# Decoder trunk: top-k selection by signs on ScalarE, and the threshold search with its branch traced ahead of the gated attention

## The chip, the cores and the metric

The kernel runs on one core of a Trainium2 chip, as one launch. The metric is the device time of that launch in microseconds (us), the median over several runs. TensorE is called PE here and its weight loads PEld; VectorE is DVE, ScalarE is ACT, GpSimd is POOL, SyncE is SP.

## The reference, cut to what matters

A trunk of two layers on 1024 tokens of width 1024, with 16 meta tokens put ahead (1040 rows in all). Each layer runs two groups of heads on the same normalised stream. Group A is gated linear attention (GLA), four heads in chunks. Group B is sparse attention: an indexer scores all earlier keys for every query, the 256 best are kept, and softmax attention runs over those. Both outputs are gated, concatenated and projected.

```python
def _layer(h, ...):
    proj = jnp.einsum('bld,de->ble', h, w_in)
    g_q, g_k, g_v, g_lr, g_z, a_q, a_k, a_v, i_q, i_k, i_w, a_z = _split_cols(proj)
    o_gla = _gla(gq, gk, gv, glog) ...          # group A, chunks of 64
    o_dsa = _dsa(aq, ak, av, iq, ik, i_w, S) * silu(a_z)
    y = concat([o_gla, o_dsa]) @ w_out
    return _layer_norm(DEEPNORM_ALPHA * h + y, ln_g, ln_b)

def one_block(inp):                             # 128 queries of _dsa
    dots = einsum('bqjd,bsd->bqjs', iqb, ik) * (IDX_HD ** -0.5)
    score = einsum('bqj,bqjs->bqs', iwb * (IDX_HEADS ** -0.5), relu(dots))
    score = where(causal, score, -inf)
    _, sel = lax.top_k(score, topk)             # topk = 256
    ...                                         # softmax over the 256 keys kept
```

## The kernel before, in words

Everything is float32, with each float32 factor split into a rounded part and a remainder, so that one projection is three passes on PE. The whole layer lives in on-chip memory; DRAM scratch holds projections that are needed in another layout.

The stages of a layer, in the order in which they are written:

- **index scores**: index projections, `index_scores` (PE dots, ACT Relu at L535, DVE weighted sum at L540) give `score[i]` for the query blocks i = 1 to 7, side by side in the tile `r_sc`; block i has 144 + 128 i columns (272, 400, ... 1040; 4592 in all).
- **GLA**: `gla_proj(f)` for the two halves f = 0, 1 (projections `wgqk` at L353 to L355 and `gvp` at L567 to L569), and `gla(f)`: a short chunk of 16 tokens, then two of 512. For each of up to seven levels DVE subtracts (L622, L624), ACT takes exponentials (L625, L628), POOL multiplies (L626, L632), PE multiplies into the tile `lev` (L639), and DVE copies under a mask (L643). The results go to `go` and `ms`.
- **attention projections**: `wak`, `waq`, `wav` (`proj_fm`, L353 to L355), with rotary embedding. The gates `wz` (`proj_z`) come from the same lines; they are traced between the attention's units at every second unit (`ZX`).
- **threshold search**, DVE: statistics of each score row, then five rounds of counts over all seven blocks (`count`, L753) with a secant step of [128x7] operations between them (L809 to L819), then `finish` (L772, L774, L776: the eight largest remaining values give the exact threshold). A matmul by ones (`fail`, L824) says whether any row still misses its count by more than 8. A branch inside a `tile_critical` (L828) repeats the search bit by bit in that case. All engines take part in that branch: DVE waits for the other engines and for the DMA queues, loads the flag, compares, and lets the others go on.
- **selection** (L861 to L873): for each block DVE counts the scores above the threshold (L866), marks the ties (L867), numbers them with a scan (L868), keeps the first ones (L870) and writes a 0/1/2 code into the score (L871); POOL scales it to a bias in bf16 (L872) and adds the causal mask (L873).
- **attention**: `va` and `ak` are made ready (transposes `vT` at L885, the split of `ak` at L896 and L897), then 32 units of two heads: `stage_a` (PE scores `S` at L1022, DVE adds the bias at L1023 and reduces, ACT exponential at L1029) and `stage_b` (PE transposes `PT` at L1047, ACT and DVE split them at L1050 and L1051, PE `o` at L1053 and later).
- **output projection and LayerNorm.**

The order on each engine is not the written one: a scheduler orders the instructions of all engines by priority and by its own estimate of when operands are there. Priority follows the written order; `tc.high_priority(offset=...)` moves a piece ahead. Each engine then runs its own list strictly in order. The search is written behind the attention projections with an offset of 1 (`TPRI`); DVE gets to it early since its operands are there, and its instructions end up among those of GLA.

Of the kernel before, what the change touches and what calls it, by code (L numbers as in the profile page):

```python
# [24 lines left out]
L = 1040  # L25
# [71 lines left out]
def trunk(ctx: ExitStack, tc, a, out, dbg=None, stop=None):  # L97
# [82 lines left out]
    V.memset(halves, 0.0)  # L180
    for o in range(2):
        V.memset(halves[64 * o:64 * o + 64, o:o + 1], 1.0)
    zcol = small(2)
    V.memset(zcol[:, 0:1], 0.0)
    V.memset(zcol[:, 1:2], 1.0)
    zero_b = zcol[:, 0:1]
# [222 lines left out]
    for l in range(DEPTH):  # L409
# [296 lines left out]
        s1 = slot(0, F32, "rope")
        ropeb = [s1[:, 520 * x:520 * x + 520] for x in range(2)]
        proj_fm(proj_dram(wfm[AK], ak_dram, 0, "wak"))
        rope_dram(ak_dram, 0, ropeb[0], KRA)
        for j in range(4):  # L710
            proj_fm(proj_dram(wfm[AQ + j], aq_dram, j, "waq", -0.125))
            rope_dram(aq_dram, j, ropeb[1 - j % 2], KRA)
        avr = s1[:, 2 * L:3 * L]

        def ev(c, n, p):
            S.activation(avr[:, c:c + n], p, AF.Copy)
        proj_fm((wfm[AV], 128, "wav", ev))

        def proj_z(j):
            def ev(c, n, p):  # L720
                if j < 4:
                    gt = unit("zu")[:, :n]
                    Q.dma_start(gt, g_dram[j, :, c:c + n])
                if j in ZDVE:
                    e = unit("zu")
                    V.tensor_scalar(e[:, :n].bitcast(I32), p.bitcast(I32), -(1 << 31), None, OP.bitwise_or)
                    S.activation(e[:, :n], e[:, :n], AF.Exp)
                    S.activation(e[:, :n], e[:, :n], AF.Ln, bias=one_b, scale=1.0)
                else:
                    e = log_sigmoid_parts(p, 0.0, 128, n, "zu")  # L730
                V.scalar_tensor_tensor(e[:, :n], p, 0.0, e[:, :n], OP.min, OP.subtract)
                S.activation(e[:, :n], e[:, :n], AF.Exp)
                if j < 4:
                    V.scalar_tensor_tensor(e[:, :n], p, ng, e[:, :n], OP.mult, OP.mult)
                    G.tensor_tensor(e[:, :n], e[:, :n], gt, OP.mult)
                else:
                    V.tensor_tensor(e[:, :n], p, e[:, :n], OP.mult)  # L737
                S.dma_start(z_dram[j, :, c:c + n], e[:, :n])
            proj_fm((wfm[GZ + j], 128, "wz", ev))

        for j in ZORD[:ZPRE]:
            proj_z(j)


        bias = {0: causal}
        for i in range(1, NB):
# [40 lines left out]
            V.tensor_tensor(sel_v, sel_v, selcap, OP.min)  # L787
            dr()

        with tc.high_priority(offset=TPRI):  # L790
            mean, sd, sl, sl_lo, sl_hi, dl = sel_w[5:11]
            th, er = sel_t, sel_e
            for i in blks:
                V.bn_stats(sel_st[:, i - 1, :], score[i][:, :min(SELN, 16 + 128 * i)])
                V.bn_aggr(sel_mv[:, i - 1, :], sel_st[:, i - 1:i, :])
            S.activation(sd, sel_mv[:, :, 1], AF.Ln, bias=eps_c, scale=1.0)
            S.activation(sd, sd, AF.Exp, scale=0.5)
            V.tensor_tensor(mean, sd, selz, OP.mult)
            V.tensor_tensor(th[0], sel_mv[:, :, 0], mean, OP.add)
            V.tensor_tensor(sl, sd, selc, OP.mult)  # L800
            V.tensor_scalar(sl_lo, sl, 0.25, None, OP.mult)
            V.tensor_scalar(sl_hi, sl, 4.0, None, OP.mult)
            for k in range(NSEC):
                t, e = th[k % 2], er[k % 2]
                count(e, t, OP.is_ge, 0.5 - TOPK)
                if k == NSEC - 1:
                    break
                nt, ok = th[1 - k % 2], sel_w[11]
                V.scalar_tensor_tensor(ok, e, -1.0, e, OP.mult, OP.max)  # L809
                V.tensor_scalar(ok, ok, 8.0, None, OP.is_lt)  # L810
                if k:
                    V.scalar_tensor_tensor(sl, er[1 - k % 2], 0.25, e, OP.add, OP.subtract)
                    V.reciprocal(sl, sl)
                    V.tensor_tensor(sl, sl, dl, OP.mult)
                    V.tensor_tensor(sl, sl, sl_lo, OP.max)
                    V.tensor_tensor(sl, sl, sl_hi, OP.min)
                V.tensor_tensor(dl, e, sl, OP.mult)
                V.tensor_tensor(nt, t, dl, OP.add)
                V.copy_predicated(nt, ok.bitcast(I32), t)  # L819

            V.scalar_tensor_tensor(sel_w[11], e, -1.0, e, OP.mult, OP.max)
            V.scalar_tensor_tensor(sel_w[11], sel_w[11], 8.0, selact, OP.is_gt, OP.mult)
            pf = tr("fail")
            T.matmul(pf[:, :7], ones, sel_w[11], start=True, stop=True)  # L824
            finish(e)
            V.tensor_reduce(sel_w[11][:1, 0:1], pf[:1, :7], axis=AX.X, op=OP.max)
            V.tensor_scalar(sel_f, sel_w[11][:1, 0:1], 0.0, None, OP.is_gt)
            with tc.tile_critical(sync_engine=mybir.EngineType.DVE):  # L828
                left = V.value_load(sel_f)
                with V.If(left != 0):  # L830

                    cnt, neg, acc, z0 = er[0], er[1], sel_w[11], sel_w[10]
                    mt, ct = th[0].bitcast(I32), th[1].bitcast(I32)
                    V.memset(z0, 0.0)
                    V.drain()
                    count(cnt, z0, OP.is_ge, 0.0)
                    V.drain()
                    V.tensor_scalar(neg, cnt, float(TOPK), None, OP.is_lt)
                    V.drain()
                    V.tensor_copy(mt, neg)  # L840
                    V.drain()
                    V.tensor_scalar(mt, mt, 31, None, OP.logical_shift_left)
                    V.drain()
                    for bit in range(30, -1, -1):
                        V.tensor_scalar(ct, mt, 1 << bit, None, OP.bitwise_or)
                        V.drain()
# [12 lines left out]
            cnt = er[0]
            for i in blks:  # L860
                W = 144 + 128 * i  # L861
                t = sel_v[:, i - 1:i]
                rr[5] = 1 - rr[5]
                oz = r_oz[:, rr[5]]
                eq, cs = oz[:, :260].bitcast(U8), oz[:, 260:780].bitcast(I16)
                V.tensor_scalar(bias[i], score[i], t, float(-TOPK), OP.is_gt, OP.add, accum_out=cnt[:, i - 1:i])  # L866
                V.tensor_scalar(eq[:, :W], score[i], t, None, OP.is_equal)  # L867
                V.tensor_tensor_scan(cs[:, :W], eq[:, :W], zero_b.to_broadcast([128, W]), cnt[:, i - 1:i],  # L868
                                     OP.add, OP.add)
                V.scalar_tensor_tensor(eq[:, :W], cs[:, :W], 0.0, eq[:, :W], OP.is_gt, OP.mult)  # L870
                V.scalar_tensor_tensor(score[i], score[i], t, eq[:, :W], OP.is_lt, OP.add)  # L871
                G.tensor_scalar(bias[i], score[i], BIG, 0.0, OP.mult, OP.add)  # L872
                G.tensor_tensor(bias[i][:, W - 128:W], bias[i][:, W - 128:W], causal[:, 16:144], OP.add)  # L873

        vat = [slot(1, F32R, "va"), slot(3, F32R, "vb")]
        va = []
# [305 lines left out]
def _tables():  # L1182
# [24 lines left out]
    for p in range(128):  # L1207
        for i in range(1, NB):
            nv = 17 + 128 * i + p
            z = NormalDist().inv_cdf(max(5e-3, 1 - TOPK / nv))  # L1210
            seltab[p, i - 1] = z
            seltab[p, 6 + i] = np.sqrt(2 * np.pi) / (nv * max(np.exp(-z * z / 2), 0.15))
            seltab[p, 13 + i] = BIG if nv >= TOPK else -BIG
            seltab[p, 20 + i] = nv >= TOPK
    seltab[:, 28:] = np.arange(8) + 0.5
    return {"ident": np.eye(128, dtype=np.float32), "causal": causal, "mcaus": mcaus, "lmask": lmask,
# [43 lines left out]
```

## Time and profile before

| | us |
|---|---|
| median of 3 runs | 1513.29 (1512.71 to 1514.68) |
| profiled execution, its own time | 1515.28 |
| span of that execution | 1513.5 |
| PE busy | 1386.8 (92%) |
| DVE busy | 1061.5 (70%) |
| ACT busy | 762.6 (50%) |
| POOL busy | 723.3 (48%) |

PE is the busiest engine. "Busy" counts the time in which an instruction of the engine ran; a group line gives the engine, the operation, output and input tiles with their sizes, the count, the busy time and the mean of one in ns, and behind the second bar the idle time just before, with what ended it. The granted clock (PEclk) is given as a share of 2.4 GHz: 1.00 is that level throughout, 0.5 is 1.2 GHz.

### The profile page before, as it was taken

Reading aid. Unit: us, or ns where it says so; the run is one execution under the profiler, and the core shown is the slowest. Engines: PE = TensorE matmul, PEld = TensorE weight load, DVE = VectorE, ACT = ScalarE, POOL = GpSimd, SP = SyncE. Lnnn points to the kernel's source line nnn. Section 1 sums busy time; section 2 is a strip of 40 time slices with the busy share of each in tenths; the row PEclk is TensorE's granted clock in tenths of the full one; section 3 lists DMA queues with packets and bytes.
Section 4 is the critical chain, followed back from the end, with each engine's and each line's share of the span. In section 5 each row is a group of like instructions: output and inputs, shape, how many; then the busy total and the mean of one; then the engine's idle time right before and its main releaser. Section 6 shows DMA issues by size and latency. Waiting matters only on the chain. (4 is left out here: it accounts for less than half of the span.)

```text
span 1513.5 us, 27140 instructions
## 1 busy us (share of the span) xinstructions
PE 1386.8 (92%) x9471; PEld 1290.6 (85%) x9471; DVE 1061.5 (70%) x2465; ACT 762.6 (50%) x1745; POOL 723.3 (48%) x690
## 2 busy tenths in 40 slices
PE   2988998999968999999999899999997899999985
PEld 2888897898958998898998889888897799899985
DVE  8569999565197556776497699994624955778638
ACT  5446623343355777653254573334434577876412
POOL 6533346596344546322363442866923644652134
PEclk9999999999978999999999999999998899999988
DMA  7242331242423446215233432314242253631422
GB/s 250 102 141 82 91 116 50 86 127 83 129 64 92 136 132 163 66 48 158 75 126 116 124 98 81 107 58 127 83 131 64 65 147 106 183 109 52 153 67 112
DMA packets 143166, 162.63 MB, mean 107 GB/s; under 512 B 19552, under 2 KB 112496, under 8 KB 143024
## 3 DMA queue, kind: packets, MB, share of 16 engines
q1 hardware_dynamic: 112656, 125.73, 27.9%
q10 hardware_dynamic: 30368, 35.12, 6.8%
q8 instruction: 75, 1.23, 0.3%
q14 instruction: 67, 0.55, 0.1%
HBM read 104.76 MB, written 56.04 MB: 106 GB/s over the span
## 5 line engine op out<-in xcount | busy, mean ns | idle before, releaser
L320 POOL TENSOR_TENSOR w<-w 128x512 fp32r<-128x512 f32 (+1 forms) x134 | 179.4, 1339 | 299.6 <-ACT w L319 232.5
L319 ACT ACTIVATE w<-w 128x512 fp32r<-128x512 f32 (+1 forms) x134 | 83.4, 624 | 108.7 <-DMA w<-in_w_fm_dram 58.4
L353 PE MATMUL wz<-X,w 128*128 128x346 f32 (+1 forms) x384 | 130.5, 340 | 2.3 <-DVE zu L737 1.8
L540 DVE SCALAR_TENSOR_TENSOR r_sc<-v,cst,r_sc 128x346 f32<-128x346 f32 (+6 forms) x196 | 125.0, 693 | 6.3 <-ACT v L535 5.2
L354 PE MATMUL wz<-X,w 128*128 128x346 f32 (+1 forms) x384 | 129.3, 337 | 0.0
L355 PE MATMUL wz<-X,w 128*128 128x346 f32 (+1 forms) x384 | 129.3, 337 | 0.0
L1051 DVE TENSOR_TENSOR u<-PT,u 128x512 fp32r<-128x512 f32 (+1 forms) x160 | 100.4, 632 | 30.1 <-ACT u L1050 21.3
L1050 ACT ACTIVATE u<-PT 128x512 fp32r<-128x512 f32 (+1 forms) x160 | 85.9, 544 | 61.9 <-PE PT L1047 60.4
L1029 ACT ACTIVATE r_g<-r_g,cst 128x272 f32<-128x272 f32 (+7 forms) x128 | 99.7, 779 | 20.1 <-DVE cst L1023 19.8
L632 POOL TENSOR_TENSOR qb<-r_g,u 64x256 f32<-64x256 f32 (+1 forms) x144 | 104.2, 724 | 5.8
L1022 PE MATMUL S<-ak,aq 128*128 128x346 f32 (+7 forms) x240 | 81.9, 348 | 18.8 <-DVE ak L897 10.3
L567 PE MATMUL gvp<-w,X 128*128 128x256 f32 (+1 forms) x288 | 83.3, 291 | 9.5 <-DVE r_g L643 8.0
L535 ACT ACTIVATE v<-dots 128x346 f32<-128x346 f32 (+5 forms) x224 | 85.8, 457 | 12.2 <-PE dots L533 8.5
L1047 PE MATMUL PT<-cst,r_g 128*128 128x128 f32 x576 | 89.2, 278 | 1.1 <-DVE cst L1023 1.1
L568 PE MATMUL gvp<-w,X 128*128 128x256 f32 (+1 forms) x288 | 83.4, 290 | 0.0
L569 PE MATMUL gvp<-w,X 128*128 128x256 f32 (+1 forms) x288 | 82.8, 288 | 0.0
L353 PEld LDWEIGHTS wz<-X,w 128*128 128x128 f32 x384 | 76.4, 199 | 3.9 <-DVE zu L737 2.3
L354 PEld LDWEIGHTS wz<-X,w 128*128 128x128 f32 x384 | 76.7, 200 | 0.3
L355 PEld LDWEIGHTS wz<-X,w 128*128 128x128 f32 x384 | 76.4, 199 | 0.4
L1117 PE MATMUL yp<-w,X 128*128 128x256 f32 (+1 forms) x238 | 69.9, 295 | 6.0 <-ACT X L1087 6.0
L643 DVE COPY_PREDICATED r_g<-cst,lev 128x512 f32<-128x512 uint8 (+1 forms) x72 | 52.5, 729 | 32.0 <-PE lev L639 31.4
L1022 PE MATMUL S<-ak 128*128 128x346 f32 (+7 forms) x240 | 74.8, 320 | 0.0
(348 smaller groups left out, 4900.6 us busy)
## 6 DMA issues: line engine op xcount, KB each, us to landing
w<-in_w_fm_dram SPq DMA_DIRECT2D x88, 256.0 KB
r_g<-aq_dram SPq DMA_DIRECT2D x64, 128.0 KB
w<-in_w_out_dram SPq DMA_DIRECT2D x32, 256.0 KB
r_sc<-h_dram SPq DMA_DIRECT2D x53, 128.0 KB
h_dram<-r_g SPq DMA_DIRECT2D x12, 512.0 KB
r_dram<-r_sc SPq DMA_DIRECT2D x48, 128.0 KB
r_sc<-z_dram SPq DMA_DIRECT2D x22, 256.0 KB
z_dram<-zu ACTq DMA_DIRECT2D x32, 173.0 KB
```

The costliest lines, as they stand in the source:

```text
L320: G.tensor_tensor(lo[:, :n], raw[:, :n], hi[:, :n].bitcast(F32), OP.subtract)
L353: T.matmul(p[:m, :n], wh, xh, start=(k == 0), stop=False)
L354: T.matmul(p[:m, :n], wh, xl, start=False, stop=False)
L355: mm = T.matmul(p[:m, :n], wl, xh, start=False, stop=(k == 7))
L535: S.activation(rl[:, :n], p[:, :n], AF.Relu)
L540: V.scalar_tensor_tensor(sco[:, c:c + n], rl[:, :n], w, sco[:, c:c + n], OP.mult, OP.add)
L632: eng.tensor_tensor(qb[P, :, o].rearrange("p c (b m) -> p c b m", m=m), qv[P, :, 1, :].rearrange("p (c b) m -> p c b m", c=nch), Ev[P, :, ...
L1022: mm = T.matmul(p[:, :n], q[x][:, h % 4, :], ak[g][:, c:c + n], start=(x == 0), stop=(x == 1))
L1029: ins = S.activation(P[:, :W], P[:, :W], AF.Exp, bias=mx[:, h, nci - 1:nci], scale=-1.0, accum_out=mx[:, h, 4:5]).ins
L1047: T.transpose(p[:, 256 * x + 128 * hh:256 * x + 128 * hh + 128], Pt[hh][:, 128 * (k0 + x):128 * (k0 + x) + 128], ident)
L1050: S.activation(ph[:, :256 * kk], p[:, :256 * kk], AF.Copy)
L1051: V.tensor_tensor(pl[:, :256 * kk], p[:, :256 * kk], ph[:, :256 * kk].bitcast(F32), OP.subtract)
```

## The change

1. **The search moves.** Search and branch become a function that is called right behind the index scores, ahead of `gla_proj(0)`; all of GLA and the attention projections are written behind it. The `fail` matmul, its reduction and the branch get an offset of 4000 (`FPRI`), and `fail` has a PSUM bank of its own.
2. **The selection changes.** For each block ACT takes the sign of score minus threshold (with its sum) and the square of the sign (with its sum); two DVE operations of [128x1] work out how many ties fit; a DVE scan numbers the ties from these (bf16 in, minus one per column that isn't a tie); one DVE operation joins sign and number into an integer; ACT turns it into the bias with a Relu scaled by minus `BIG`. POOL has no part any more. Causally masked columns carry a score of about minus `BIG`, so their sign masks them. The selection stays behind the projection code, with an offset of 1 (`SELPRI`).

```diff
+SELPRI = 1
+FPRI = 4000
...
-    zcol = small(2)
+    zcol = small(3)
+    V.memset(zcol[:, 2:3], -1.0)
...
-        gla_proj(0)
-        gla(0)
-        gla_proj(1)
-        gla(1)
...
-        with tc.high_priority(offset=TPRI):
+        def search():
+            with tc.high_priority(offset=TPRI):
+                search_()
+
+        def search_():
...
-            pf = tr("fail")
-            T.matmul(pf[:, :7], ones, sel_w[11], start=True, stop=True)
+            with tc.high_priority(offset=FPRI):
+                pf = bank("fl", 1, "fail")
+                T.matmul(pf[:, :7], ones, sel_w[11], start=True, stop=True)
             finish(e)
-            V.tensor_reduce(sel_w[11][:1, 0:1], pf[:1, :7], axis=AX.X, op=OP.max)
-            V.tensor_scalar(sel_f, sel_w[11][:1, 0:1], 0.0, None, OP.is_gt)
-            with tc.tile_critical(sync_engine=mybir.EngineType.DVE):
+            with tc.high_priority(offset=FPRI):
+                V.tensor_reduce(sel_w[11][:1, 0:1], pf[:1, :7], axis=AX.X, op=OP.max)
+                V.tensor_scalar(sel_f, sel_w[11][:1, 0:1], 0.0, None, OP.is_gt)
+            with tc.high_priority(offset=FPRI), tc.tile_critical(sync_engine=mybir.EngineType.DVE):
...
+        search()
+        gla_proj(0)
+        gla(0)
+        gla_proj(1)
+        gla(1)
...
+        with tc.high_priority(offset=SELPRI):
+            negt, sums, room = sel_w[10], sel_w[8:10], sel_w[7]
+            V.tensor_scalar(negt, sel_v, -1.0, BIG / 2, OP.mult, OP.min)
             for i in blks:
...
-                V.tensor_scalar(bias[i], score[i], t, float(-TOPK), OP.is_gt, OP.add, accum_out=cnt[:, i - 1:i])
-                V.tensor_scalar(eq[:, :W], score[i], t, None, OP.is_equal)
-                V.tensor_tensor_scan(cs[:, :W], eq[:, :W], zero_b.to_broadcast([128, W]), cnt[:, i - 1:i],
-                                     OP.add, OP.add)
-                V.scalar_tensor_tensor(eq[:, :W], cs[:, :W], 0.0, eq[:, :W], OP.is_gt, OP.mult)
-                V.scalar_tensor_tensor(score[i], score[i], t, eq[:, :W], OP.is_lt, OP.add)
-                G.tensor_scalar(bias[i], score[i], BIG, 0.0, OP.mult, OP.add)
-                G.tensor_tensor(bias[i][:, W - 128:W], bias[i][:, W - 128:W], causal[:, 16:144], OP.add)
+                S.activation(sg, score[i], AF.Sign, bias=negt[:, x], scale=1.0, accum_out=sums[0][:, x])
+                S.activation(ne, sg, AF.Square, accum_out=sums[1][:, x])
+                V.tensor_scalar(room[:, x], sums[0][:, x], sums[1][:, x], -0.5, OP.add, OP.mult)
+                V.tensor_scalar(room[:, x], room[:, x], float(TOPK), None, OP.add)
+                V.tensor_tensor_scan(left[:, :W], ne, zcol[:, 2:3].to_broadcast([128, W]), room[:, x], OP.add, OP.add)
+                V.scalar_tensor_tensor(left[:, :W], sg, 2048.0, left[:, :W], OP.mult, OP.add)
+                S.activation(bias[i], left[:, :W], AF.Relu, scale=-BIG)
...
-            seltab[p, 13 + i] = BIG if nv >= TOPK else -BIG
+            seltab[p, 13 + i] = BIG if nv >= TOPK else -BIG / 2
```

What this does to the order on the engines is shown in three places. An UNCONDITIONAL_BRANCH is the point at which an engine enters the branch of the search.

**DVE, in the search of layer 0.** Before, between the counts (L753) and the secant steps (L809 and on) stand GLA's operations (L604 to L643):

```order
L753 TENSOR_SCALAR r_kb,cst<-r_sc,cst 128x1040
L604 TENSOR_TENSOR r_g<-cst,dg 16x2x16
L622 TENSOR_TENSOR u<-r_g 128x4x64
L624 TENSOR_TENSOR u<-r_g 128x4x64
L622 TENSOR_TENSOR u<-r_g 128x8x32
L624 TENSOR_TENSOR u<-r_g 128x8x32
L643 COPY_PREDICATED r_g<-cst,lev 16x2x8
L809 SCALAR_TENSOR_TENSOR cst<-cst 128x7
L812 SCALAR_TENSOR_TENSOR cst<-cst 128x7
```

After, the search runs through to the branch with nothing of GLA in it (L733 to L746 are its `finish`, L794 loads the flag):

```order
L733 SCALAR_TENSOR_TENSOR r_oz<-r_sc,cst,r_kb 128x1040
L735 MAX r_kb<-r_oz 128x8
L740 TENSOR_TENSOR r_kb<-r_kb 128x56
L742 TENSOR_REDUCE cst<-r_kb 128x7
L744 TENSOR_TENSOR cst<-cst 128x7
L746 TENSOR_TENSOR cst<-cst 128x7
L793 NO_OP
L1266 UNCONDITIONAL_BRANCH
L794 TENSOR_LOAD cst
L795 COMPARE_AND_BRANCH
```

All of GLA on DVE now stands behind the branch, together with the selection (L871 to L883 of the changed kernel).

**PE, around the branch of layer 0.** Before, the branch stands among the gates `wz`, just ahead of the transposes for the attention:

```order
L353 MATMUL wz<-X,w 128x346
L1255 UNCONDITIONAL_BRANCH
L885 MATMUL vT<-cst,rope 128x128 x8
L885 MATMUL vT<-cst,rope 16x128
L354 MATMUL wz<-X,w 128x346
L355 MATMUL wz<-X,w 128x346
```

After, it stands among the `gvp` matmuls of the second half, ahead of GLA's first matmul (`dg`):

```order
L571 MATMUL gvp<-w,X 128x256
L1266 UNCONDITIONAL_BRANCH
L572 MATMUL gvp<-w,X 128x256
L606 MATMUL dg<-cst,u 16x2
L642 MATMUL lev<-qb,r_g 16x16 x2
L660 MATMUL khT<-cst,u 16x128
L570 MATMUL gvp<-w,X 128x256
```

Ahead of the branch stand now all 216 `gvp` of the first half, the 144 `wgqk` of the second and 131 of its `gvp` (136 in layer 1). Behind it stand 85 `gvp` (80), all matmuls of GLA, 432 of `wak`, `waq` and `wav`, 66 of `wz` (74) and the nine `vT`, and then the first `S`. After the last `go` of GLA 51 `wz` are left ahead of that `S` in layer 0, and 6 in layer 1. Before, 96 `wz` stood ahead of the first `S`, 35 of them behind the branch. `fail` stands two matmuls ahead of the end of `wgqk` in layer 0, two behind it in layer 1.

**ACT, behind the branch of layer 0.** After, it has two small exponentials, then the seven Sign (L877), two Square (L878) and a `gvp` eviction ahead of GLA's first exponential over 512 columns (L628). The end of that row of work:

```order
L877 ACTIVATE r_kb,cst<-r_sc,cst 128x784
L878 ACTIVATE r_oz,cst<-r_kb 128x272
L575 ACTIVATE zu<-gvp 128x512
L877 ACTIVATE r_kb,cst<-r_sc,cst 128x912
L877 ACTIVATE r_kb,cst<-r_sc,cst 128x1040
L878 ACTIVATE r_oz,cst<-r_kb 128x400
L661 ACTIVATE r_g<-khT 16x128
L655 ACTIVATE cst<-r_g 128x4
L628 ACTIVATE u<-u 128x512
```

Before, ACT had nothing of the selection; behind its branch stood the gates' activations (L404 to L406) and the copy of `vT`.

Instruction counts: POOL 28 fewer, DVE 11 fewer, ACT 42 more, PE and SP the same.

## Rows read from the trace of the kernel before

**Rows 1.** The page: busy time, share of the span and instructions of each engine
```profile
PE 1386.8 (92%) x9471; PEld 1290.6 (85%) x9471; DVE 1061.5 (70%) x2465; ACT 762.6 (50%) x1745; POOL 723.3 (48%) x690
```

**Rows 2.** Windows: stretch, length, busy of PE PEld DVE ACT POOL, clock, DMA share, GB/s
```profile
209.70:260.00 50.30, 44.11 (x297) 40.47 (x296) 49.80 (x109) 16.59 (x35) 37.70 (x43) 0.93 0.29 90
260.00:415.10 155.10, 154.96 (x1075) 141.18 (x1074) 73.71 (x126) 60.07 (x127) 92.19 (x107) 1.00 0.35 104
415.10:480.00 64.90, 45.24 (x241) 42.03 (x242) 56.37 (x105) 32.39 (x85) 32.44 (x27) 0.79 0.24 69
947.00:1000.00 53.00, 47.73 (x344) 44.82 (x344) 52.69 (x117) 18.27 (x40) 37.63 (x46) 0.97 0.26 82
1150.20:1210.00 59.80, 43.37 (x219) 40.34 (x219) 52.34 (x97) 30.09 (x77) 28.59 (x25) 0.77 0.20 59
190.00:200.00 10.00, 10.00 (x87) 10.00 (x86) 9.29 (x35) 1.97 (x5) 0.00 (x0) 1.00 0.18 56
400.00:410.00 10.00, 10.00 (x65) 10.00 (x64) 1.32 (x4) 2.77 (x7) 3.60 (x3) 1.00 0.28 70
```
The first and the fourth stretch begin with GLA's first matmul (`dg`), the third and the fifth where PE stops for the branch. From 190 to 200 us PE runs `gvp` alone, from 400 to 410 `wav` and `wz` alone.

**Rows 3.** Waits of PE, 209.7 to 480 us (layer 0): total, times, longest
```profile
PE S L1022 <- DVE cst L1023: 5.7, 2, 5.1
PE gvp L567 <- DVE r_g L643: 5.6, 2, 4.0
...
PE o L1054 <- DVE u L1051: 2.6, 2, 1.4
```

**Rows 4.** Waits of PE, 947 to 1210 us (layer 1)
```profile
PE S L1022 <- DVE ak L897: 5.3, 1, 5.3
PE vT L885 <- DVEq L828: 4.1, 1, 4.1
...
PE o L1054 <- DVE u L1051: 2.3, 1, 2.3
```

**Rows 5.** Timeline of PE from the branch of layer 0: start, length, wait before
```profile
419.17 1.66 PE L885 MATMUL vT<-cst,rope 128*128 128x128 f32 x9 [4.10 <-DVEq L828]
...
420.91 0.49 PE L355 MATMUL wz<-X,w 128*128 128x346 f32 x1
...
422.93 0.44 PE L353 MATMUL wz<-X,w 128*128 128x346 f32 x1
...
432.54 0.46 PE L1022 MATMUL S<-ak,aq 128*128 128x144 f32 x1 [5.01 <-DVE ak L897]
```

**Rows 6.** Groups of DVE, 190 to 282 us: the search of layer 0
```profile
L753 DVE TENSOR_SCALAR_CACHE_REDUCE r_kb<-r_sc,cst 128x272 bf16<-128x272 f32 (+6 forms) x35 | 29.0, 892 | 0.1
...
L774 DVE SCALAR_TENSOR_TENSOR r_oz<-r_sc,cst,r_kb 128x272 f32<-128x272 f32 (+6 forms) x7 | 7.2, 1054 | 0.0
L776 DVE MAX8 r_kb<-r_oz 128x8 f32<-128x272 f32 (+6 forms) x7 | 5.6, 829 | 0.0
L772 DVE TENSOR_SCALAR r_kb<-r_kb,cst 128x272 bf16<-128x272 bf16 (+6 forms) x7 | 4.6, 724 | 0.0
```

**Rows 7.** Timeline of DVE: the search's first steps, layers 0 and 1
```profile
191.26 0.17 DVE L798 TENSOR_TENSOR cst<-cst 128x7 f32<-128x7 f32 x1 [0.61 <-ACT cst L797]
191.34 0.16 DVE L800 TENSOR_TENSOR cst<-cst 128x7 f32<-128x7 f32 x1
...
928.29 0.17 DVE L798 TENSOR_TENSOR cst<-cst 128x7 f32<-128x7 f32 x1 [0.61 <-ACT cst L797]
```

**Rows 8.** Groups of DVE, 418 to 475 us, and of ACT and DVE, 415 to 475
```profile
L868 DVE TENSOR_TENSOR_SCAN r_oz<-r_oz,cst 128x272 int16<-128x272 uint8 (+6 forms) x7 | 13.6, 1972 | 0.0
...
L896 ACT ACTIVATE ak<-r_g 128x1040 fp32r<-128x1040 f32 x2 | 2.0, 1056 | 0.0
...
L897 DVE TENSOR_TENSOR ak<-r_g,ak 64x1040 fp32r<-64x1040 f32 x2 | 2.4, 1236 | 0.0
```

**Rows 9.** Timelines of DVE and PE: GLA's second half begins; its last `ms`
```profile
301.82 0.17 DVE L604 TENSOR_TENSOR r_g<-cst,dg 16x32 f32<-16x32 f32 x1 [3.86 <-PE dg L603]
...
391.21 1.02 PE L692 MATMUL ms<-v,cst 128*128 128x512 f32 x2
```

More of the change, by code (lines that the diff above doesn't have):

```diff
@@ L698, in gla @@
                                 oc.rearrange("p (h t) -> p h t", h=2))
-        gla_proj(0)
-        gla(0)
-        gla_proj(1)
-        gla(1)
[L706 to L742, printed above, removed]
         bias = {0: causal}
@@ L857, in trunk @@
                     finish(cnt, V.drain)
-            cnt = er[0]
+        search()
[3 more added lines that the diff above has]
+        gla(1)
+        s1 = slot(0, F32, "rope")
+        ropeb = [s1[:, 520 * x:520 * x + 520] for x in range(2)]
+        proj_fm(proj_dram(wfm[AK], ak_dram, 0, "wak"))
+        rope_dram(ak_dram, 0, ropeb[0], KRA)
+        for j in range(4):
+            proj_fm(proj_dram(wfm[AQ + j], aq_dram, j, "waq", -0.125))
+            rope_dram(aq_dram, j, ropeb[1 - j % 2], KRA)
@@ new lines, in trunk, with ev, proj_z @@
+        avr = s1[:, 2 * L:3 * L]
+        def ev(c, n, p):
+            S.activation(avr[:, c:c + n], p, AF.Copy)
+        proj_fm((wfm[AV], 128, "wav", ev))
+        def proj_z(j):
+            def ev(c, n, p):
+                if j < 4:
+                    gt = unit("zu")[:, :n]
+                    Q.dma_start(gt, g_dram[j, :, c:c + n])
+                if j in ZDVE:
+                    e = unit("zu")
+                    V.tensor_scalar(e[:, :n].bitcast(I32), p.bitcast(I32), -(1 << 31), None, OP.bitwise_or)
+                    S.activation(e[:, :n], e[:, :n], AF.Exp)
+                    S.activation(e[:, :n], e[:, :n], AF.Ln, bias=one_b, scale=1.0)
+                else:
+                    e = log_sigmoid_parts(p, 0.0, 128, n, "zu")
+                V.scalar_tensor_tensor(e[:, :n], p, 0.0, e[:, :n], OP.min, OP.subtract)
+                S.activation(e[:, :n], e[:, :n], AF.Exp)
+                if j < 4:
+                    V.scalar_tensor_tensor(e[:, :n], p, ng, e[:, :n], OP.mult, OP.mult)
+                    G.tensor_tensor(e[:, :n], e[:, :n], gt, OP.mult)
+                else:
+                    V.tensor_tensor(e[:, :n], p, e[:, :n], OP.mult)
+                S.dma_start(z_dram[j, :, c:c + n], e[:, :n])
+            proj_fm((wfm[GZ + j], 128, "wz", ev))
@@ L860, in trunk @@
+        for j in ZORD[:ZPRE]:
+            proj_z(j)
+        with tc.high_priority(offset=SELPRI):
+            negt, sums, room = sel_w[10], sel_w[8:10], sel_w[7]
+            V.tensor_scalar(negt, sel_v, -1.0, BIG / 2, OP.mult, OP.min)
             for i in blks:
-                W = 144 + 128 * i
-                t = sel_v[:, i - 1:i]
+                W, x = 144 + 128 * i, slice(i - 1, i)
                 rr[5] = 1 - rr[5]
-                oz = r_oz[:, rr[5]]
-                eq, cs = oz[:, :260].bitcast(U8), oz[:, 260:780].bitcast(I16)
@@ L872, in trunk @@
-                G.tensor_scalar(bias[i], score[i], BIG, 0.0, OP.mult, OP.add)
-                G.tensor_tensor(bias[i][:, W - 128:W], bias[i][:, W - 128:W], causal[:, 16:144], OP.add)
+                sg, oz = bias[i], r_oz[:, rr[5]]
+                left, ne = oz[:, :520].bitcast(I16), oz[:, 520:].bitcast(BF16)[:, :W]
+                S.activation(sg, score[i], AF.Sign, bias=negt[:, x], scale=1.0, accum_out=sums[0][:, x])
+                S.activation(ne, sg, AF.Square, accum_out=sums[1][:, x])
```

## The prediction

> **What bounds the kernel now.** I read the busy times first: PE works 1386.8 us of the span, DVE 1061.5, ACT and POOL half of it [rows 1]. PE works in order, so a change is worth the time in which PE stands still or runs at its lower clock, and nothing else. So I looked next for such places, by windows [rows 2]. There are two in each layer, and between them PE is full: 154.96 of 155.10 us at clock 1.00. The first place is the start of GLA (209.7 to 260, and 947 to 1000). DVE does the threshold search there and GLA's subtractions and masked copies in turn; PE waits for a masked copy (L643) for 5.6 us [rows 3], and the granted clock falls to 0.93 and 0.97. The second is the branch and what follows it (415.1 to 480, and 1150.2 to 1210). PE waits 4.1 us for the branch, then 5.0 or 5.3 for the `ak` that DVE makes between selection blocks, 5.7 in layer 0 for the masked scores, and 2.6 or 2.3 for the split of `PT` [rows 3 to 5]. PE works 45.24 us of 64.9 there at a mean clock of 0.79, and 43.37 of 59.8 at 0.77. After the branch the records show it directly: seven matmuls start 0.289 us apart from 420.91 to 422.93 [rows 5], where the same kind takes 10.00/65 = 0.154 at clock 1.00 [rows 2]. The clock is at its 1.2 GHz level for a while after each stop, then at 2.4 GHz again.
>
> **What there is to win.** Stops: 50.30 − 44.11 = 6.2 and 53.00 − 47.73 = 5.3 at the start of GLA; 64.90 − 45.24 − 4.1 = 15.6 and 59.80 − 43.37 − 4.1 = 12.3 at the attention, the branch itself left out since it stays. Together 39.4. Lower clock, as busy time × (1 − granted clock): 3.1 + 1.4 + 9.5 + 10.0 = 24.0. The sum is **63.4**; it is an upper bound, since some of it is the attention's own.
>
> **Part by part, what is kept or new.**
>
> *The search alone on DVE, and the branch.* It starts at 191.26 [rows 7]. Its operations add up to 29.0 for the counts and 4.6 + 7.2 + 5.6 for the finish, 46.4 [rows 6]; about 70 small ones and the 35 sums read out start 0.08 apart [rows 7], 8.4 more. So DVE reaches the branch 54.8 us later, at 246.1. PE has 144 `wgqk` at 0.154 and 131 `gvp` at 10.00/87 = 0.115 to do from 209.7, where GLA began [rows 2]: 209.7 + 22.2 + 15.1 = 247.0. In layer 1 DVE starts at 928.29 [rows 7] and is there at 983.1; PE needs 947.0 + 22.2 + 15.6 = 984.8 [rows 2]. They arrive together, so PE's loss is the branch's own 4.1 [rows 4, 5], as now, and I charge 1 us a layer for the later one: **2**. If DVE were 5 us late it would be 10. `fail` needs the fifth count, some 36 us after the start (29.0 and the small ones), so 227; PE gets to it at 209.7 + 22.2 = 231.9, and five us of cover are enough.
>
> *Restart.* The stop of 4.1 us will bring the 1.2 GHz level for some us, as it did behind the old branch. There seven matmuls lost 0.135 each, 0.9 us, and the transposes ahead of them ran in it too [rows 5]. I charge 2 a layer: **4**. The rest of the 19.5 us of lower clock at the attention came from the further stops there, and goes with them.
>
> *Start of GLA.* It now starts behind the branch, with the whole machine at rest. ACT does seven Sign and two Square first. The nearest row is ACT's copy of 1040 columns, 1.06 us [rows 8]; 4592 columns of Sign and 672 of Square are then 5.4 us, and with their sums read, the `gvp` eviction and the small ones I take 9.8. PE has 78 `gvp` ahead of the first large `lev`, 9.0 us. So PE comes to it a little early, and the levels then come at POOL's pace. DVE does the selection beside it: a scan and one joined operation per block, by the old scan 13.6 [rows 8] and by L774 of the same widths 7.2 [rows 6], about 21 us in all, against the 36 us of search that stood behind 209.7. On SP's queue the first loads of `h` wait for the Signs of the two longest blocks, whose columns they overwrite, and the loads of `gk`, `gv` and four weights are behind them. Bounds are nothing, and twice what the start costs today. I take what it costs today, stops and clock of the two windows: 6.2 + 5.3 + 3.1 + 1.4 = **16.0**, for the search leaves DVE, but Signs, queue and selection come in.
>
> *The selection leaves the attention.* Old L866 to L873 no longer stand between `va` and `ak`. The waits for the split of `PT`, 2.6 + 2.3, belong to the attention's own first small tiles and stay: **4.9**. `ak` can be loaded only when GLA's last `go` has read its place. Behind that stand 51 `wz` in layer 0, 7.9 us, against 2 × 1.06 + 2 × 1.24 = 4.6 [rows 8] and a load; in layer 1 only 6, 0.9 us, and there PE will wait. I charge 1 + 5: **6** (bounds 0 and 10).
>
> *What is hidden.* From restart to the first `S` PE has 85 × 0.115 + 498 × 0.154 + 1.7 for `vT`, and the matmuls of GLA. Those I get from the windows: PE did 44.11 + 154.96 = 199.1 from 209.7 to 415.1, of which 216 `gvp`, 576 of `wgqk`, `wak`, `waq` and `wav` and 61 `wz` make 122.9, and 3.1 is clock; 73 is left. In all 161 us. POOL had 37.70 + 92.19 = 129.9 in that stretch and loses some weight splits to the time ahead of the branch; DVE had 49.80 + 73.71 = 123.5 and loses the search behind 209.7. ACT gains 10 for the Signs and more for Square and Relu, on 76.7. All stay below 161. If that cover fails, rival C follows.
>
> **The sum.** 63.4 − 2 − 4 − 16.0 − 4.9 − 6 = 30.5 us won. The profiled execution took 1515.28, so 1484.8; it stands 2.0 above the median of 1513.29, so the forecast is **1483**.
>
> **Rivals.**
>
> *A, all of it goes.* Start of GLA, restart and `ak` cost nothing, only 2 + 4.9 stay: 56.5 won, 1457. For it: nothing but Signs is on ACT. Against: every stop in these rows left a low clock behind it.
>
> *B, the Signs hold the start of GLA longer.* One engine feeds the level exponentials and the selection. If Sign and the reading of its sum cost much more than a plain copy, or the loads are late, the start costs twice what I charge: 1483 + 16 = 1499. The trace has ACT's copy of 1040 columns at 1.06 us, against 1.24 for a DVE operation with two inputs on as many columns [rows 8]. The Trainium skill, ScalarE: Activation LUTs, section Rules for kernel authors, speaks against the change: relu, max, add and the like belong on VectorE, up to some three times faster per element in bf16. Taken whole, three times my 5.4 us is 11 more a layer, an estimate of 1505 by that page; these rows, with float32 scores, show no such gap.
>
> *D, the attention's start stays slow.* The first units have small tiles, 144 and 272 columns, with a chain through DVE, ACT and PE each; the waits for L1023 [rows 3] may be theirs and not the selection's, and with them the low clock. Then about 22 of the 47.4 counted there remain: 1505.
>
> *C, slower: GLA becomes the bound.* It now runs in a stretch with 161 us of PE work, and took 181.5 from its first `dg` (209.7) to its last `ms` (391.21) [rows 2, 9], the first half 92.1 (to 301.82). Were both halves as long, with the Signs ahead and 4 us of `wz` behind, the way from restart to the first `S` is 184.2 + 9.8 + 4 = 198. My forecast has 161 + 2 + 8 + 3 = 174. So 24 a layer more: 1531. It decides from 174 + 15 = 189 on, since 15 a layer is what I win. For it: DVE was busy 49.80 of the first 50.30 us, and POOL, which does all of a level's multiplications, was busy 92.19 of 155.10 [rows 2]. Against: in that stretch PE was full, so PE's order and not GLA's chain set most of the 181.5.
>
> That the change doesn't do what it says I leave out: the orders show search, branch and selection where it puts them.
>
> **How the numbers follow.** Forecast 0.51; B 0.18, as its price is a new one on the path; D 0.12; A 0.08; C 0.11, of which 0.03 ends near break-even. About 0.2%, 3 us, is what a measurement of this kernel can tell from no change. Faster: 0.51 + 0.18 + 0.12 + 0.08 = 0.89; same 0.03; slower 0.08. The range leaves out C and half of A: from 1460, between A and the forecast, to 1507, just past D.
>
> **What would show it.** Right: DVE and PE meet at the branch near 247 and 985 us, with one wait of about 4; from there to the first `S` PE's stops add up to under 10 us a layer; the first `S` of layer 0 starts near 247 + 4 + 174 = 425 instead of 432.54 [rows 5]; no selection in the attention, and a clock near 1.00 in its first 60 us. Wrong: waits of PE for `lev` or for DVE and POOL behind the branch above 15 us a layer, DVE late at the branch, or the waits of [rows 3] for L1023 still there.

## The result, and the profile after

The changed kernel takes **1479.7 us** (median of 4 runs, 1476.5 to 1481.6) against 1514.0 before: ratio **0.9765, interval 0.9741 to 0.9789**. Measured a second time on another occasion, it gave 0.9753 (0.9739 to 0.9766). The forecast was 1483, with a range from 1460 to 1507. The profiled execution took 1479.79, 35.5 us less than the one before. All ratios here are of runs at the usual clock; one run, of the kernel without the branch (1664 us at a mean granted clock of 0.75), is left out of them.

The page of the changed kernel, busy time of each engine, to be put beside [rows 1]:

```profile
PE 1377.4 (93%) x9471; PEld 1283.4 (87%) x9471; DVE 1040.1 (70%) x2440; ACT 791.7 (54%) x1815; POOL 721.3 (49%) x662
```

No engine has much less to do. What went is time in which PE stood or ran slowly. The windows show where (stretch, length, busy of PE, PEld, DVE, ACT, POOL, granted clock, DMA share, GB/s), to be put beside [rows 2]; the last two are the attention's start in the two layers:

```profile
209.70:247.20 37.50, 37.48 (x271) 36.69 (x269) 35.40 (x85) 8.08 (x15) 11.07 (x8) 1.00 0.27 88
247.20:413.00 165.80, 153.98 (x1024) 137.37 (x1025) 106.57 (x174) 76.97 (x170) 124.92 (x137) 0.95 0.32 97
968.00:1060.00 92.00, 81.26 (x549) 73.93 (x549) 66.03 (x107) 46.23 (x105) 73.38 (x82) 0.93 0.33 101
413.00:480.00 67.00, 66.95 (x432) 62.85 (x429) 31.70 (x95) 53.42 (x140) 28.61 (x24) 1.00 0.44 124
1142.00:1200.00 58.00, 58.00 (x375) 54.21 (x373) 28.91 (x91) 45.00 (x122) 20.77 (x17) 1.00 0.44 125
```

During the search PE is now full (37.48 of 37.50), and from 413 us on it is full at clock 1.00, where it had worked 45.24 of 64.9 us at 0.79. What is left of the loss lies between the branch and the end of GLA. PE's waits from 200 to 480 us (layer 0), to be put beside [rows 3]:

```profile
PE lev L642 <- POOL qb L635: 5.4, 2, 4.3
PE dg L606 <- DVEq L793: 4.0, 1, 4.0
PE go L670 <- DVE r_g L646: 1.1, 1, 1.1
PE waq L358 <- POOL w L323: 0.9, 1, 0.9
PE wak L358 <- POOL w L323: 0.4, 1, 0.4
```

and from 930 to 1200 (layer 1), to be put beside [rows 4]:

```profile
PE lev L642 <- POOL qb L635: 5.8, 3, 4.4
PE dg L606 <- DVEq L793: 4.7, 1, 4.7
PE wak L358 <- POOL w L323: 0.6, 1, 0.6
```

Nothing waits for L1034 (the old L1023), for `ak` or for the split of `PT` any more; one engine is named that in these stretches had no wait of weight before (0.5 and 0.3 us for `lev`): POOL. The timeline around the branch of layer 0 (start, length, wait), DVE first, then PE, with the first `S`:

```profile
245.72 0.17 DVE L746 TENSOR_TENSOR cst<-cst 128x7 f32<-128x7 f32 x1
251.26 0.17 DVE L871 TENSOR_SCALAR cst<-cst 128x7 f32<-128x7 f32 x1 [5.38 <-DVEq L793]
```
```profile
246.91 0.27 PE L572 MATMUL gvp<-w,X 128*128 128x256 f32 x1
251.16 0.22 PE L606 MATMUL dg<-cst,u 128*16 128x2 f32 x2 [3.98 <-DVEq L793]
...
425.91 0.34 PE L1033 MATMUL S<-ak,aq 128*128 128x144 f32 x2
```

DVE ends its search at 245.9 (forecast 246.1), PE its matmuls at 247.2 (247.0), and `S` begins at 425.9 (425).

### The profile page after: what moved, and what is told of

It reads as the page before. It is cut to its first block, busy times and chain, and to the rows that moved or that the text cites. A ratio compares the mean times of both kernels' runs of the same rounds, so it can differ in the third digit from the quotient of the medians.

```text
span 1478.0 us, 27238 instructions
## 1 busy us (share of the span) xinstructions
PE 1377.4 (93%) x9471; PEld 1283.4 (87%) x9471; DVE 1040.1 (70%) x2440; ACT 791.7 (54%) x1815; POOL 721.3 (49%) x662
## 5 line engine op out<-in xcount | busy, mean ns | idle before, releaser
L356 PE MATMUL wz<-X,w 128*128 128x346 f32 (+1 forms) x384 | 125.9, 328 | 0.3
L357 PE MATMUL wz<-X,w 128*128 128x346 f32 (+1 forms) x384 | 125.0, 326 | 0.0
L358 PE MATMUL wz<-X,w 128*128 128x346 f32 (+1 forms) x384 | 124.6, 324 | 0.0
L635 POOL TENSOR_TENSOR qb<-r_g,u 64x256 f32<-64x256 f32 (+1 forms) x144 | 114.9, 798 | 5.6
L629 POOL TENSOR_TENSOR r_g<-r_g,u 128x256 f32<-128x256 f32 (+1 forms) x60 | 49.6, 826 | 67.9 <-PE lev L642 40.5
L642 PE MATMUL lev<-qb,r_g 128*128 128x128 f32 (+1 forms) x480 | 66.8, 277 | 11.2 <-POOL qb L635 11.2
L642 PEld LDWEIGHTS lev<-qb,r_g 128*128 128x128 f32 (+1 forms) x480 | 60.0, 189 | 17.9 <-POOL qb L635 12.7
L1034 DVE CUSTOM_DVE_ANT_0 r_g<-S,r_kb 128x456 f32<-128x456 f32 (+6 forms) x112 | 55.9, 519 | 27.1 <-PE S L1033 20.2
```

The source lines that it names most:

```text
L356: T.matmul(p[:m, :n], wh, xh, start=(k == 0), stop=False)
L357: T.matmul(p[:m, :n], wh, xl, start=False, stop=False)
L358: mm = T.matmul(p[:m, :n], wl, xh, start=False, stop=(k == 7))
L635: eng.tensor_tensor(qb[P, :, o].rearrange("p c (b m) -> p c b m", m=m), qv[P, :, 1, :].rearrange("p (c b) m -> p c b m", c=nch), Ev[P, :, ...
L642: T.matmul(pv[:, ch], kst, qb[:, ch], start=True, stop=True)
```

## The experiments

All ratios are to the kernel before, measured in the same session. Two theories stood against each other. By mine from the prediction, what stops PE behind the branch is the head of ACT's work, Signs ahead of GLA's exponentials. By the one that the profile after suggests, it is POOL, which is slowed by DVE's scans beside it.

**Either half of the change alone.** First the search moved, with the old selection (L866 to L873 before) in the place of the new one:

```diff
         with tc.high_priority(offset=SELPRI):
...
-                S.activation(sg, score[i], AF.Sign, bias=negt[:, x], scale=1.0, accum_out=sums[0][:, x])
...
-                S.activation(bias[i], left[:, :W], AF.Relu, scale=-BIG)
+                V.tensor_scalar(bias[i], score[i], t, float(-TOPK), OP.is_gt, OP.add, accum_out=cnt[:, i - 1:i])
...
+                G.tensor_tensor(bias[i][:, W - 128:W], bias[i][:, W - 128:W], causal[:, 16:144], OP.add)
...
```

> The changed kernel with the old selection (DVE and POOL, five and two operations per block) in the place of the new one; search and branch stay ahead of GLA. If moving the search is what wins, most of the 34 us remain: 1480 to 1492 us. If the new selection is needed for it, because the old one puts 39.6 us of DVE and 12.2 us of POOL per layer into the start of GLA, where POOL was busy 9.7 of every 10 us in the changed kernel's trace from 260 to 300 us, each layer loses about the 12 us of POOL: 1500 to 1510 us.

Measured 0.9950 (0.9933 to 0.9968), 1510.4 us: only a fifth of the gain, at the end of the second expectation. Its windows behind the branch (columns as above):

```profile
260.00:280.00 20.00, 17.67 (x129) 16.99 (x129) 20.00 (x32) 6.99 (x13) 17.23 (x18) 1.00 0.33 105
280.00:300.00 20.00, 14.89 (x81) 13.96 (x81) 20.00 (x16) 4.25 (x13) 17.98 (x14) 0.83 0.20 60
300.00:320.00 20.00, 16.09 (x90) 15.05 (x88) 19.93 (x20) 5.54 (x10) 19.27 (x18) 0.83 0.27 86
```

DVE is the third number of busy time and full for sixty us; POOL, the last, has 54.5 of these 60, and PE 48.7. The old selection's 40 us of DVE and 12 of POOL are not hidden there, they stand in GLA's way: apart from the branch PE waits most for POOL's `qb`, 4.9 us in layer 0 and 7.7 in layer 1. Which of the two engines' work costs how much, this run doesn't show. Then the new selection with search and branch in the old place:

```diff
-                V.tensor_scalar(bias[i], score[i], t, float(-TOPK), OP.is_gt, OP.add, accum_out=cnt[:, i - 1:i])
...
-                G.tensor_tensor(bias[i][:, W - 128:W], bias[i][:, W - 128:W], causal[:, 16:144], OP.add)
+                S.activation(sg, score[i], AF.Sign, bias=negt[:, x], scale=1.0, accum_out=sums[0][:, x])
...
+                S.activation(bias[i], left[:, :W], AF.Relu, scale=-BIG)
...
```

> The kernel before with the new selection by signs, but search and branch in the old place behind the projections. If the selection's length on DVE was what held the attention's start, it goes from 39.6 us to about 21 per layer and half of the 47 us counted there return: 1488 to 1500 us. If the place of branch and selection is what counts, PE still stops for the branch, then for a chain of Sign, Square, scan, joined operation and Relu per block: 1505 to 1515 us.

Measured 1.0053 (1.0037 to 1.0070): slower than before, by 8 us, and outside both expectations. Its windows behind the branch:

```profile
420.00:440.00 20.00, 13.48 (x76) 12.82 (x75) 14.49 (x34) 19.03 (x52) 7.11 (x5) 0.84 0.31 92
440.00:460.00 20.00, 12.18 (x55) 10.39 (x56) 19.72 (x35) 16.07 (x41) 9.37 (x6) 0.67 0.27 79
```

Here ACT is full (19.03 of 20) where it was not before: the attention's exponentials, the gates' and 21 operations of the selection meet. Yet the 8 us are not lost here. The search of layer 1 begins at 927.85, against 928.29 before [rows 7], so layer 0 cost nothing. They are lost in layer 1. PE's first matmul behind the branch there and its first `S`, in the kernel before and then in this one:

```profile
1154.36 2.18 PE L885 MATMUL vT<-cst,rope 128*128 128x128 f32 x9 [4.14 <-DVEq L828]
...
1169.25 0.46 PE L1022 MATMUL S<-ak,aq 128*128 128x144 f32 x1 [5.31 <-DVE ak L897]
```
```profile
1158.14 1.97 PE L887 MATMUL vT<-cst,rope 128*128 128x128 f32 x9 [4.46 <-DVEq L829]
...
1176.45 0.89 PE L1024 MATMUL S<-ak,aq 128*128 128x144 f32 x3 [4.51 <-DVE ak L899]
```

So 3.8 us are lost ahead of the branch, in GLA, where PE waits 5.4 us for the masked copy that a `go` needs; why that wait came up is not shown. Another 3.4 are lost from the branch to the first `S`, where ACT is busy for 16.35 of 18.4 us (10.66 of 16 before); that ACT's work is the reason fits this, but no run shows it.

So one half gives −0.5%, the other +0.5%, and both together −2.4%. The new place pays only with the new selection, and the new selection only in the new place.

**What the selection still costs.**

```diff
-        with tc.high_priority(offset=SELPRI):
...
-                S.activation(bias[i], left[:, :W], AF.Relu, scale=-BIG)
+        rr[5] = 1 - rr[5]
```

> The changed kernel without any selection: the bias is what the search left there, so the masked keys differ; all else is in place. It shows what the whole selection costs behind the branch. If it is what stops PE at the start of GLA (stops of 7.9 and 6.4 us in the two layers behind the branch, and about 9 us of lower clock after them), some 12 to 20 us go: 1460 to 1468 us. If GLA's start stops PE by itself, through POOL's own multiplications and weight splits, 0 to 4 us go: 1476 to 1480 us.

Measured 0.9642 (0.9623 to 0.9662), as the first expectation has it. So 0.0111 to 0.0123 of the time, 17 to 19 us, is the price of the new selection behind the branch; without it PE's stops there are 0.2 us in layer 0 and 1.9 in layer 1, apart from the branch.

**Is it ACT?**

```diff
+                S.activation(sg, score[i], AF.Sign, bias=negt[:, x], scale=1.0)
                 S.activation(sg, score[i], AF.Sign, bias=negt[:, x], scale=1.0, accum_out=sums[0][:, x])
```

> The changed kernel with each Sign done twice, 5.8 us more of ACT per layer right behind the branch, ahead of GLA's first large exponential. If ACT's Signs hold the start of GLA, as my prediction had it, PE's stops there grow by about as much: 1479.7 + 2 x 5 to 6 = 1489 to 1492 us. If POOL holds it, stretched by DVE's scans beside it, ACT has room: 1479 to 1483 us.

Measured 0.9780 (0.9749 to 0.9811), which cannot be told from the changed kernel; the 9 to 12 us more of the first theory, 0.983 and above, lie outside the interval. PE's stops behind the branch, without the branch's own, came to 9.0 and 9.7 us, against 7.8 and 6.4: some more, and nearly all of them for POOL. So ACT's 5.8 us per layer do not come back in full; the runs further on, in which all Signs stay and most of the stops go, show that the Signs are not what holds the start.

**Is it the scans, and where?** The scans are held back until PE has done two of the query projections, in a second run (`HOLD = 14`) until nearly all of them; `behind` lets an instruction be ordered only after the k-th projection on PE, here counted from the first `waq`:

```diff
+HOLD = 6
...
-                V.tensor_tensor_scan(left[:, :W], ne, zcol[:, 2:3].to_broadcast([128, W]), room[:, x], OP.add, OP.add)
+                sc_ = V.tensor_tensor_scan(left[:, :W], ne, zcol[:, 2:3].to_broadcast([128, W]), room[:, x], OP.add, OP.add)
+                behind(sc_.ins, HOLD, waq0)
```

> The changed kernel with the seven scans (and the joined operations and Relus that need them) held until PE has done two of the four query projections; the Signs stay at the branch, search and branch too. DVE then scans beside GLA's third to fifth chunk instead of its first large one. If the scans beside POOL's multiplications are what stops PE at GLA's start (POOL's half-width multiplication took 961 ns there, 767 without a selection), the 6.7 and 5.6 us of stops for POOL go and some come back later, where PE has more matmuls between levels: ratio to before 0.968 to 0.973. If Sign and Square on ACT hold it, nothing changes: 0.976. If DVE's work is the same loss wherever it stands beside GLA: 0.976 too, with the stops moved.

> As the run before, but held until nearly the end of the attention projections, so that the scans follow GLA's last levels; POOL was busy only 3.3 of 20 us there in the changed kernel. If the scans beside POOL are the loss, it comes close to the run without a selection (ratio 0.964): 0.964 to 0.969. If the attention's start then waits for the scans on DVE, as in the kernel before, S waits for ak or for the mask again: 0.975 to 0.985.

Measured 0.9739 (0.9714 to 0.9763) and 0.9702 (0.9675 to 0.9730). The first is between the two expectations and its interval touches that of the changed kernel: the stops for POOL fell to 1.3 and 3.1 us, but PE now waits for `go` 3.5 and 1.8 us further on. The second lies between its expectations as well, a gain of 8 to 9 us; it leaves 2.4 us at a `go` that DVE serves late. Later is better, but some of the loss stays in either place.

**Is it that DVE is busy, or what its scan reads?** Each scan is replaced by two operations of DVE that read one operand from memory:

```diff
-                V.tensor_tensor_scan(left[:, :W], ne, zcol[:, 2:3].to_broadcast([128, W]), room[:, x], OP.add, OP.add)
+                lb = oz[:, :520].bitcast(BF16)[:, :W]
+                for _ in range(2):
+                    V.tensor_scalar(lb, ne, 0.0, 0.0, OP.is_gt, OP.add, accum_out=sel_w[6][:, x])
```

> The changed kernel with each scan replaced by two operations of DVE with one input from memory and a sum, about 0.9 us each and so about as long together (1.9 us for the scan); the ties aren't numbered. If the scan slows POOL because both of its operands and POOL's come from the same memory port, POOL's half-width multiplication falls back from 961 towards 770 to 800 ns at GLA's start and most of the stops go: ratio 0.966 to 0.971. If it is only that DVE is busy and its subtractions come late, the stops stay: 0.975 to 0.978.

Measured 0.9651 (0.9627 to 0.9676), all but the same as without a selection. PE's waits for `lev` fall to 0.4 us in layer 0 and to none in layer 1, though POOL's half-width multiplications came down only to 852 ns, not to the 770 to 800 expected. And then the real scan, with its constant operand moved from SBUF to PSUM, and nothing else changed but a small memset that fills it:

```diff
+            mone = bank("fl", 1, "mone")
+            V.memset(mone[:, 0:1], -1.0)
...
-                V.tensor_tensor_scan(left[:, :W], ne, zcol[:, 2:3].to_broadcast([128, W]), room[:, x], OP.add, OP.add)
+                V.tensor_tensor_scan(left[:, :W], ne, mone[:, 0:1].to_broadcast([128, W]), room[:, x], OP.add, OP.add)
```

> The changed kernel, with the scan's second operand, the constant minus one, held in the accumulator memory (PSUM) instead of the main one (SBUF); nothing else changes, and the order on PE is the same. If it is the scan's two operands from SBUF that slow POOL, as the stand-in with one input suggests, POOL's half-width multiplication at GLA's start falls from 961 to 770 to 850 ns, PE's stops for POOL go, and the result is still the reference's: ratio 0.964 to 0.969. If the stand-in won because it numbered nothing or was a little shorter (1.66 against 1.88 us), nothing changes: 0.975 to 0.978.

> The changed kernel unaltered, on the same chip as the run before it: 0.9765, as first measured, by every theory. It gives the comparison with the run above its own base.

Measured **0.9672 (0.9651 to 0.9693), 1468.9 us**, beside 0.9753 (0.9739 to 0.9766), 1479.1 us, for the changed kernel in the same session. This version beats both kernels. PE's waits for `lev` are 0.6 us in layer 0 and 2.9 in layer 1, against 5.4 and 5.8 in the changed kernel. Windows from 260 to 300 us, of the changed kernel, of the one with the one-operand stand-in and of the one with the constant in PSUM, in this order:

```profile
260.00:300.00 40.00, 33.23 (x220) 31.61 (x218) 34.07 (x43) 20.74 (x43) 38.38 (x30) 0.91 0.31 96
```
```profile
260.00:300.00 40.00, 39.31 (x279) 36.60 (x279) 39.75 (x70) 22.38 (x46) 36.14 (x37) 1.00 0.34 105
```
```profile
260.00:300.00 40.00, 38.23 (x271) 35.78 (x271) 37.38 (x51) 22.95 (x47) 34.28 (x35) 1.00 0.34 100
```

In the second DVE is busy for 39.75 of 40 us, more than in the first, and PE hardly stops: so DVE's being busy is not the loss. The groups of POOL and DVE from 247 to 305 us (count, busy, mean ns) of the changed kernel; the second line is the first without its four small multiplications:

```profile
L635 POOL TENSOR_TENSOR qb<-r_g,u 64x256 f32<-64x256 f32 (+1 forms) x20 | 19.2, 961 | 0.8
...
L635 POOL TENSOR_TENSOR qb<-r_g,u 64x256 f32<-64x256 f32 x16 | 17.7, 1105 | 0.6
...
L650 POOL TENSOR_TENSOR u<-u,r_g 128x512 f32<-128x512 f32 x1 | 2.9, 2924 | 0.1
...
L882 DVE TENSOR_TENSOR_SCAN r_oz<-r_oz,cst 128x272 int16<-128x272 bf16 (+6 forms) x7 | 13.2, 1880 | 0.7 <-DVE cst L881 0.5
```

and of the one with the constant in PSUM:

```profile
L635 POOL TENSOR_TENSOR qb<-r_g,u 64x256 f32<-64x256 f32 (+1 forms) x24 | 18.7, 780 | 1.0
...
L635 POOL TENSOR_TENSOR qb<-r_g,u 64x256 f32<-64x256 f32 x20 | 16.9, 845 | 0.8
...
L650 POOL TENSOR_TENSOR u<-u,r_g 128x512 f32<-128x512 f32 x1 | 1.3, 1281 | 2.2 <-ACT u L649 2.2
...
L884 DVE TENSOR_TENSOR_SCAN r_oz<-r_oz,cst,mone 128x272 int16<-128x272 bf16 (+6 forms) x7 | 11.0, 1574 | 0.7 <-ACT v L693 0.5
```

POOL does 24 multiplications in the stretch in which it did 20, those of 64x256 in 845 instead of 1105 ns, its product over 512 columns falls from 2.92 to 1.28 us, and the scan is shorter, 1.57 against 1.88 us. The Trainium skill, GPSIMD Engine Reference, section Specifications, says that POOL shares its SBUF interface with VectorE and is in contention with DVE instructions that have two SBUF inputs. The runs agree, with these numbers; they add that a constant of one column, broadcast along the scan, counts as such an input.

Single instructions show that the two engines hold up each other. First the scans over 784 and 912 columns and POOL's product in the changed kernel, then the same with the constant in PSUM, and last a scan with the constant in SBUF while POOL stands idle, in the run without the branch that follows below:

```profile
276.61 2.32 DVE L882 TENSOR_TENSOR_SCAN r_oz<-r_oz,cst 128x784 int16<-128x784 bf16 x1
...
280.56 2.33 DVE L882 TENSOR_TENSOR_SCAN r_oz<-r_oz,cst 128x912 int16<-128x912 bf16 x1
...
281.06 2.92 POOL L650 TENSOR_TENSOR u<-u,r_g 128x512 f32<-128x512 f32 x1
```
```profile
276.08 1.83 DVE L884 TENSOR_TENSOR_SCAN r_oz<-r_oz,cst,mone 128x784 int16<-128x784 bf16 x1
...
279.17 2.11 DVE L884 TENSOR_TENSOR_SCAN r_oz<-r_oz,cst,mone 128x912 int16<-128x912 bf16 x1
...
279.77 1.28 POOL L650 TENSOR_TENSOR u<-u,r_g 128x512 f32<-128x512 f32 x1 [2.23 <-ACT u L649]
```
```profile
297.17 1.85 DVE L852 TENSOR_TENSOR_SCAN r_oz<-r_oz,cst 128x784 int16<-128x784 bf16 x1
...
300.87 2.52 POOL L323 TENSOR_TENSOR w<-w 128x512 fp32r<-128x512 f32 x1 [11.31 <-DMA w<-in_w_fm_dram]
```

Beside the scan from SBUF, POOL's product ends 1.1 us behind the scan's end (282.89); beside the scan with the constant in PSUM it runs through while the scan is still at work. And the scan does not gain by reading PSUM as such: with POOL idle, the one from SBUF takes 1.85 us over 784 columns, the one with PSUM 1.83 beside a working POOL.

**What the branch costs.** The changed kernel without the branch and the repeated search in it:

```diff
-            with tc.high_priority(offset=FPRI), tc.tile_critical(sync_engine=mybir.EngineType.DVE):
-                left = V.value_load(sel_f)
-                with V.If(left != 0):
...
-                    finish(cnt, V.drain)
```

> The changed kernel without the branch and the repeated search in it (the search itself, the fail matmul and the flag stay). It measures what the branch costs where it stands now. My prediction has 4.1 us of stop and 2 us of lower clock per layer, so 12 us less, 0.8%: ratio 0.968. If GLA's start can also begin earlier without it, since nothing stops the engines and GLA's first work can stand beside the end of the search, more: 0.960 to 0.966. If GLA's start is bound by POOL and DVE all the same, less than 6 us: 0.973 to 0.976.

Measured 0.9769 (0.9738 to 0.9800), nearest to the third expectation: nothing is gained, though the stops of 4.0 and 4.7 us are gone. Its first windows show why:

```profile
209.70:247.20 37.50, 35.00 (x242) 32.73 (x241) 36.82 (x89) 13.88 (x30) 32.09 (x37) 0.99 0.38 114
247.20:260.00 12.80, 10.00 (x70) 8.28 (x69) 12.80 (x24) 2.12 (x5) 6.65 (x8) 0.90 0.07 24
```

POOL is busy 32.09 of 37.5 us during the search, against 11.07 with the branch: the scheduler lets GLA in beside the search again, as before the change, and PE waits there. The branch holds GLA back, and that is worth about what it costs.

## Why the prediction was right, and where not

- **The account of what there is to win held.** Kept, by the profile after, are stops of 7.8 and 6.4 us behind the branch (the waits listed above, without the branch's own), the lower clock there, 153.98 × 0.05 + 81.26 × 0.07 = 7.7 + 5.7, and half a us more of branch: 28.1. 63.4 − 28.1 = 35.3, and the two profiled executions differ by 35.5. So PE's stops and its granted clock in these stretches account for the whole change.
- **Search and branch**: DVE and PE met within 1.3 us, in layer 0 at the times worked out. In layer 1 they met at 967.4 and 967.5, not near 985, for there the search itself began 19.2 us earlier than before (909.06 against 928.29). PE lost the branch's own 4.0 and 4.7 us, not the 1 us a layer on top.
- **The attention's start**: I kept 4.9 us for waits of its own and 6 for `ak`. Neither came; PE is full there at clock 1.00, in layer 1 too, where only 6 `wz` stand behind the last `go`. Those 10.9 us were priced too high.
- **Restart and start of GLA**: I charged 4 + 16.0, and 14.2 + 13.4 = 27.6 was measured: 7.6 too little. At the attention and the branch I charged 10.9 and 1.5 too much. That these misses nearly cancel, and the sum of 30.5 came within 5 us of 35.3, is luck.
- **The step that failed** is the reason given for the start of GLA: "Signs, queue and selection come in", and rival B's Signs above all. Doubling the Signs cost nothing that can be told, and no wait of PE, DVE or POOL there is for a load. Of the selection it is the scan, through POOL: I compared its length on DVE (21 us against 36 of search) and did not ask what it reads. With the scan's constant in PSUM some 10 to 12 us of what is left go.
- **Rival A** (all of it goes, 1457) is near what the kernel without a selection does (0.9642, or 1460): it came close to the limit. **Rival B** named the right place and the wrong engine: ACT's work ahead of GLA's first large exponential took 7.8 us (251.14 to 258.93), where I had counted 9.8. The estimate of 1505, by the rule of the Trainium skill, ScalarE: Activation LUTs, section Rules for kernel authors, did not come about. I had multiplied ACT's own row by a ratio that the page gives between the two engines, which made that estimate wrong from the start. **Rival D** fell: the waits for L1023 were the selection's. **Rival C** did not happen, but the run with the old selection (1510) shows how near it lay: with 40 us of DVE and 12 of POOL in GLA's stretch four fifths of the gain were gone.

## What to carry to other kernels

Price a moved piece of work not by its length alone, but by what each instruction reads, where another engine works beside it: here a scan with both operands in SBUF slowed POOL, and moving one constant to PSUM brought a third as much again as the whole change. A full engine need not be the one that costs time: with the stand-in DVE was fuller than before, and PE hardly stopped. Two halves of a change can each be worth almost nothing and together 2.4%, so price them together. And look in which layer and stretch the time is lost before a full engine is blamed for it. A stop of all engines can be worth what it costs, if it keeps a scheduler from mixing two stages.

## What the runs showed of the hardware that was not expected

- A DVE scan that reads two operands from SBUF, one of them a single column broadcast, and a POOL product beside it hold up each other. In layer 0 POOL's float32 product over 512 columns took 2.92 us there (2.98 when the changed kernel was profiled again) and 1.28 with the column in PSUM; its multiplications of 64x256 took 1105 and 845 ns on average.
- The scan takes 1.57 us on average with that column in PSUM, and 1.88 with it in SBUF. This is POOL's doing and not PSUM's: over 784 columns it takes 1.83 us from PSUM, 1.85 from SBUF while POOL is idle, and 2.32 from SBUF beside POOL.
- Behind the branch, after a stop of 4.0 us, the mean granted clock was 0.73 from 247.2 to 260 us, and again, after PE's stops for POOL, 0.83 from 280 to 300 us (0.5 would be 1.2 GHz throughout):

```profile
247.20:260.00 12.80, 8.84 (x60) 8.48 (x61) 4.59 (x17) 8.83 (x26) 2.29 (x6) 0.73 0.31 87
260.00:280.00 20.00, 19.47 (x143) 18.43 (x141) 19.44 (x29) 12.24 (x29) 18.76 (x17) 1.00 0.39 123
280.00:300.00 20.00, 13.76 (x77) 13.18 (x77) 14.62 (x15) 8.49 (x16) 19.62 (x14) 0.83 0.23 69
300.00:320.00 20.00, 20.00 (x139) 16.92 (x139) 14.67 (x25) 9.54 (x20) 15.98 (x20) 1.00 0.16 52
```

So these stops cost more than their length: 6.2 us of stop from 280 to 300 bring 2.3 us of lower clock (13.76 × 0.17) with them.
